# Seven-product groups summed in the accumulator banks, in all four groups of the first stage too

## The chip, the core and the metric

One core of a Trainium2 chip runs the whole program. The metric is the device time of one execution in microseconds (us). The kernel before takes 918.64 us (median of 3 runs, 917.53 to 919.39).

## What is computed

A trunk of two layers over x of 256 tokens by 1024 channels, all in float32. Each layer has a feed-forward stage, an attention mixer and a second feed-forward stage, so there are four feed-forward stages (stage 1 to 4 below):

```python
def swiglu(h, w_gate, w_up, w_down):
    return (jax.nn.silu(h @ w_gate) * (h @ w_up)) @ w_down
...
    for l in range(DEPTH):
        x = x + 0.5 * swiglu(rms_norm(x, ffn1_norm[l]), ffn1_w_gate[l], ffn1_w_up[l], ffn1_w_down[l])
...
        x = x + jnp.concatenate([out_a, out_b], axis=-1) @ w_out[l]
        x = x + 0.5 * swiglu(rms_norm(x, ffn2_norm[l]), ffn2_w_gate[l], ffn2_w_up[l], ffn2_w_down[l])
    return rms_norm(x, final_norm)
```

`w_gate` and `w_up` are 1024 x 2816, `w_down` is 2816 x 1024.

## The kernel before

**Products.** Each operand is kept as a high part and a low part (the rest), so that one product of 128x128 by 128x512 is three matmuls: high by high, low by high, high by low. The 2816 columns of gate and up are worked through in five groups of 512 columns (`NGRP = 5`, group 0 to 4) and a last one of 256. In a plain group gate and up each take the 256 tokens (two halves of 128) by the 1024 channels (two halves of 512), that is eight products of a 128-token half with a 512x512 quarter of the weights, each of 12 matmuls. In a group by seven (`SEVEN`, L31, and `by_seven`, L637) the four quarters A (gate, upper rows), B (up, upper), C (up, lower) and D (gate, lower) and the four quarters of x are combined as in Strassen's and Winograd's scheme: seven products, with A, D, B+C, C, A+B, A+B+C and A+B+C+D as weights, and sums of x's quarters (`make_sums`, L349, four of them, in `sm`) as the other factor. The results are put together by VectorE (`put`, L642: five combinations a group) from copies that ScalarE made (`m1`, `m7`). Stage 1 has groups 2 to 4 by seven, the other stages groups 1 to 4.

**Hidden units and down projection.** Gate goes through SiLU on ScalarE (`silu`, L603), is multiplied by up on VectorE (`up`, L614) and gives h, which PE transposes (`turn`, L694) and multiplies by two blocks of `w_down` (`down`, L708) during the next group; the sums of the down projection stay in four of PSUM's eight banks (`accs`, L706) through the stage.

**Weights.** `specs` lists all loads and splits as steps in the order of their use; a step of the usual kind is 1 MiB. `emit_dma` (L148) loads into one of six buffers (`raw`) on SP's queue; `emit_split` (L191) makes high and low parts by a cast on ScalarE and a subtraction on VectorE, two halves a step, of 1.05 and 1.22 us. B+C and A+B are made by accumulating DMAs on GpSimd's queue (`gather`, L126), which read the second weight from memory and add it to the loaded buffer; A+B+C and A+B+C+D are then made in place by VectorE (`plus`, L131).

**What sets the order.** Instructions on TensorE (PE), ScalarE (ACT), VectorE (DVE) and GpSimd (POOL) are kept in program order (`Kept`, L40). `weights()` (L249) hands out the next step and calls `ahead` (L228), which issues splits up to `2 * i + look` half steps ahead, and loads up to ten steps ahead while fewer than six buffers are held; the second half of a step's use calls `ahead` again (`Split.part`, L182) unless `held`. So at each such place, casts enter ACT's queue ahead of whatever the program issues afterwards. Accumulating DMAs may be kept back in `pending` (`issue`, L165: kind 2, C onto B, with B's load; kind 1, B onto A, after A's splits) while `hold` is at least their kind; `flush` (L171) issues them, the last one first. `hold` starts at 2; it is 1 from the end of every later feed-forward stage and mixer on. In stage 1 `flush` is called by `take_x` (L441 to 466) in its third part, after the squares of x, the statistics (`stats`, L397, whose last step r is on POOL) and `constants()` (L487), which puts eight small DMAs and some small work on POOL. In the other stages it is called by `late` (L592) behind the statistics.

**Group 0** (L712 to 746): two steps a0 and b0 in parts, then d0 and c0, 72 of the matmuls after the last part of x. With `1 in sevens` it also copies x for the sums (`norm.copies`, eight ACT instructions) and makes the sums.

Of the kernel before, what the change touches and what calls it, by code (L numbers as in the profile page):

```python
# [14 lines left out]
P = 128  # L15
# [15 lines left out]
SEVEN = ((2, 3, 4), (1, 2, 3, 4))  # L31
# [3 lines left out]
def trunk(ctx: ExitStack, tc: tile.TileContext, x, n1, g1, u1, d1, nm, w_in, sink,  # L35
# [35 lines left out]
    def bank():  # L71
        return ps.tile([P, 512], F32, tag="ps", bufs=8, name=nm_("ps"))
# [19 lines left out]
    class Step:  # L92
        def __init__(self, kn, n, moves, key=None, prep=None, src=None, free=None, behind=None):
            self.kn, self.n, self.moves, self.prep = kn, n, moves, prep
            self.behind = behind
# [19 lines left out]
    def seven(wg, wu, c0, downs, first):  # L115
# [15 lines left out]
        def plus(x, to):  # L131
            def prep():
                for h in (0, 2):
                    x_, t_ = [raws[i][:, h:h + 2] for i in (x, to)]
                    dve.tensor_tensor(t_, t_, x_, op=ALU.add)
# [92 lines left out]
    def ahead(n):  # L228

        n = min(n, 2 * len(specs) - 1)  # L230
        while True:
            if at["split"] <= n and at["prep"] > at["split"] // 2:
# [3 lines left out]
            elif at["prep"] <= min(n // 2 + 1, len(specs) - 1) and at["dma"] > at["prep"] and \  # L236
                    (specs[at["prep"]].prep is None or at["split"] >= 2 * at["prep"]):
# [21 lines left out]
    for l in range(DEPTH):  # L259
        def ffn_specs(wg, wu, wd, sevens):  # L260
# [3 lines left out]
            for g in range(1, NGRP):  # L264
                downs = [down(g - 1, h) for h in range(2)]
                if g in sevens:
                    specs.extend(seven(wg[l], wu[l], g * 512, downs, g == 1))
                else:
                    specs.extend(plain(w[l], g * 512, 512, k0, 4) for w in (wg, wu) for k0 in (0, 4))
                    specs.extend(downs)  # L270
# [35 lines left out]
    class Norm:  # L306
# [42 lines left out]
        def make_sums(self):  # L349
# [19 lines left out]
            s1 = add(b1, t1, ALU.subtract)  # L369
            s2 = add(s1, t0, ALU.add)  # L370
            yield
            high(s1)
            high(s2)
            yield
            low(0, s1)
            b0_ = add(b0, s2, ALU.subtract)
            low(1, s2)
            v = add(t1, t0, ALU.subtract)
            yield
            high(b0_)  # L380
            high(v)
            yield
            low(2, b0_)
            low(3, v)
# [145 lines left out]
    def tokens(accs, xs, w, k0, ks=range(4), first=0, last=KC - 1, order=None, cols=slice(None), h=None):  # L530

        for k, t in (order or [(k, t) for k in ks for t in range(2)]):
            kk = k0 + k
            hi, lo = w.part(k, cols, h)
            xv = xs[kk // 2][:, kk % 2]
            xh, xl = xv[:, t * P:(t + 1) * P], xv[:, S + t * P:S + (t + 1) * P]
# [23 lines left out]
    def first_groups(norm, ws):  # L560

        sls = [halves(bank()) for _ in ws]
# [39 lines left out]
    def ffn(norm, aside=None, before=None, final=False, sevens=SEVEN[1]):  # L602
# [34 lines left out]
        def by_seven(h, g):  # L637
# [3 lines left out]

            def put(o, x, y, op):  # L642
                dve.tensor_tensor(o, x, y, op=op)
                return o

            late, run = g == max(sevens), 1 in sevens
            m1, m7 = flat(), flat()


            if g > 1:  # L650
                g0 = prod(norm.quarter(0, 0), weights())
                act.copy(m1, g0)
                p7 = prod(norm.summed(3), weights(1, True))
                act.copy(m7, p7)
                hT = turn(h, 2)
                prod(norm.quarter(0, 1), weights(), g0)
                p3 = prod(norm.summed(2), weights())
                if not run:
                    g0 = silu(flat(), g0, 0)
                down(hT, g - 1, 0, weights())  # L660
                if run:
                    g0 = silu(flat(), g0, 0)
            else:
                p1 = prod(norm.quarter(0, 0), weights(1, True))
                hT = turn(h, (0,))
                w = weights(1, True)
                act.copy(m1, p1)
                p2 = prod(norm.quarter(0, 1), w)
                hT += turn(h, (1,))
                g0 = put(flat(), p2, m1, ALU.add)  # L670
                down(hT, 0, 0, weights())
                silu(g0, g0, 0)
                p3 = prod(norm.summed(2), weights())
                p7 = prod(norm.summed(3), weights(1, True))
                act.copy(m7, p7)
            h = blk(F32)
            p5 = prod(norm.summed(0), weights())
            prod(norm.summed(1), weights(look[0] - 5 if late else run, late or run), p7)
            u1 = put(m1, p7, m1, ALU.subtract)
            p4 = prod(norm.quarter(1, 1), weights(look[0] - 4 if late else 3 * run, late or run))  # L680
            g1 = put(flat(), p4, u1, ALU.subtract)
            w = weights(look[0] - 3 if late else 2 * run)
            silu(g1, g1, 1)
            put(u1, u1, p5, ALU.subtract)
            u0 = put(m7, u1, m7, ALU.subtract)
# [476 lines left out]
```

## Time and profile before

| | |
|---|---|
| median of 3 runs | 918.64 us |
| profiled execution | 917.39 us |
| its span, first to last instruction | 915.6 us |
| PE busy | 904.5 us (99%) |
| DVE busy | 792.5 us (87%) |
| ACT busy | 589.8 us (64%) |
| POOL busy | 66.4 us (7%) |
| bytes moved | 200.87 MB, mean 219 GB/s |

Stretches of the profile: group 0 of stage 1 up to about 31 us, its group 1 (plain) to 65 us, three groups by seven to 157 us, the end of the stage and the mixer to 284 us, stage 2 to about 457 us, stage 3 to about 633 us, the mixer to 734 us, stage 4 to the end.

All helpers issue through one line, so the rows of the profile nearly all read L50 and are told apart by engine, operation and tiles: `w<-raw` is a split, `ps<-w,s`, `ps<-w,q` and `ps<-w,v` are products (x in `s`, its sums in `q` and `v`), `ps<-ident,s` is a transposition of h, `raw<-in_ffn_w_up_dram` on POOL is an accumulating DMA, `junk<-xk` are the squares, `tmp<-ps,r` and `tmp<-tmp,r` are SiLU, `s<-ps,gcol` of 128x256 f32 are the copies of x for the sums. A row of the timeline gives start, duration, engine, instruction, count, and in brackets the idle time of the engine before it and what ended it. Times of a busy PE include a modelled tail of the last matmul.

### The profile page before, as it was taken

How to read it: one execution, taken by the hardware profiler on the slowest of the kernel's cores; microseconds unless marked ns; L12 is line 12 of the kernel's file. 1: busy time of each engine (PE TensorE's matmuls, PEld its weight loads, DVE VectorE, ACT ScalarE, POOL GpSimd, SP SyncE). 2: the span in 40 equal slices, each digit the busy share in tenths (PEclk: the TensorE clock that was granted, in tenths of full speed). 3: DMA queues.
4: the chain of work that ended last, by engine and by line, in shares of the span. 5: the costliest groups of instructions: out<-in, count | busy, mean ns of one | idle time of the engine just before them, and what ended most of it. 6: DMA issues, size and time to landing. Idle time of an engine off the chain costs nothing.

```text
span 915.6 us, 12544 instructions
## 1 busy us (share of the span) xinstructions
PE 904.5 (99%) x4696; PEld 763.7 (83%) x4696; DVE 792.5 (87%) x1096; ACT 589.8 (64%) x917; POOL 66.4 (7%) x83
## 2 busy tenths in 40 slices
PE   8999999999999999999999999999999999999997
PEld 6888888899888888888888888888998888888886
DVE  6768999959975999999789999997797689999994
ACT  7836676557865766576486666665677496666561
POOL 0400100000010100100010010000001010010011
PEclk9999999999999999999999999999999999999999
DMA  9996898828436698898767998887463467998831
GB/s 339 355 238 173 265 297 268 238 93 240 136 108 189 158 280 248 257 273 275 258 164 201 276 285 217 265 293 219 116 230 98 139 153 201 275 289 230 259 132 47
DMA packets 114061, 200.87 MB, mean 219 GB/s; under 512 B 3662, under 2 KB 31376, under 8 KB 114000
## 3 DMA queue, kind: packets, MB, share of 16 engines
q1 hardware_dynamic: 96528, 166.74, 54.5%
q0 software_dynamic: 16096, 31.75, 19.3%
q10 hardware_dynamic: 1376, 1.57, 0.5%
q8 instruction: 37, 0.61, 0.3%
q14 instruction: 24, 0.20, 0.1%
HBM read 199.00 MB, written 1.05 MB: 218 GB/s over the span
## 4 chain that ended last, share of the span: by engine, by line
PE 98%; issue 1%; DMA 0%; ACT 0%; DVE 0%; POOLq 0%; POOL 0%; ACTq 0%
PE ps L50 98%; DMA xk<-in_x_dram 0%; ACT w L50 0%; DVE s L50 0%; DVE xk L50 0%; ACT tmp L50 0%; ACT L50 0%; POOLq L1157 0%; POOL rf L50 0%; ACTq L50 0%; DVE tot L50 0%; DVE tmp L50 0%
## 5 line engine op out<-in xcount | busy, mean ns | idle before, releaser
L50 PE MATMUL ps<-w,s 128*128 128x512 f32 (+1 forms) x2574 | 600.2, 391 | 0.5 <-ACT tmp L50 0.5
L50 PEld LDWEIGHTS ps<-w,s 128*128 128x128 f32 x2574 | 477.6, 188 | 100.3 <-ACT tmp L50 2.3
L50 DVE TENSOR_TENSOR w<-raw,w 128x1024 fp32r<-128x1024 f32 (+1 forms) x458 | 482.1, 1101 | 37.8 <-ACT w L50 36.6
L50 ACT CAST w<-raw 128x1024 fp32r<-128x1024 f32 (+1 forms) x458 | 409.8, 954 | 122.6 <-DVE raw L50 78.4
L50 PE MATMUL ps<-w,q 128*128 128x512 f32 x540 | 127.3, 389 | 0.0
L50 PEld LDWEIGHTS ps<-w,q 128*128 128x128 f32 x540 | 101.4, 188 | 21.0
L50 PE MATMUL ps<-s,w 128*128 128x256 f32 x672 | 83.1, 284 | 0.0
L50 PEld LDWEIGHTS ps<-s,w 128*128 128x128 f32 x672 | 81.5, 192 | 0.5
L50 POOL DMA_DIRECT2D raw<-in_ffn_w_up_dram x30 | 38.9, 1296 | 472.8 <-DVE w L50 240.8
L50 DVE TENSOR_TENSOR raw<-raw,raw 128x1024 f32<-128x1024 f32 x60 | 70.7, 1219 | 0.0
L50 ACT ACTIVATE s<-ps,gcol 128x256 fp32r<-128x256 f32 (+1 forms) x80 | 31.7, 480 | 43.7 <-PE ps L50 42.1
L50 ACT CAST s<-ps 128x512 fp32r<-128x512 f32 x44 | 24.3, 594 | 29.9 <-PE ps L50 29.9
L50 PE MATMUL ps<-w,v 128*128 128x512 f32 x180 | 43.3, 389 | 0.0
L50 ACT COPY tmp<-ps 128x512 f32<-128x512 f32 x34 | 19.9, 585 | 36.2 <-PE ps L50 34.0
L50 ACT ACTIVATE s<-s,negm 128x256 f32<-128x256 f32 x64 | 31.9, 500 | 14.8 <-DVE negm L50 14.8
L50 PE MATMUL ps<-ident,s 128*128 128x128 f32 x304 | 39.7, 273 | 0.0
L50 PEld LDWEIGHTS ps<-w,v 128*128 128x128 f32 x180 | 33.8, 188 | 7.0
L50 PEld LDWEIGHTS ps<-ident,s 128*128 128x128 f32 x304 | 35.1, 140 | 5.1 <-issue 0.8
L50 DVE TENSOR_TENSOR s<-ps,s 128x512 fp32r<-128x512 f32 x44 | 28.7, 686 | 9.1 <-ACT s L50 9.1
L50 DVE SCALAR_TENSOR_TENSOR s<-ps,gcol,s 128x256 fp32r<-128x256 f32 x48 | 20.3, 478 | 11.6 <-ACT s L50 11.5
L50 DVE TENSOR_TENSOR tmp<-ps,tmp 128x512 f32<-128x512 f32 x37 | 25.4, 686 | 2.7 <-PE ps L50 2.1
L50 DVE TENSOR_TENSOR xk<-xk,ps 128x512 f32<-128x512 f32 (+1 forms) x25 | 14.1, 598 | 14.9 <-PE ps L50 14.9
(106 smaller groups left out, 404.7 us busy)
## 6 DMA issues: line engine op xcount, KB each, us to landing
raw<-in_ffn_w_down_dram SPq DMA_DIRECT2D x44, 1024.0 KB, 8.9
raw<-in_ffn_w_gate_dram SPq DMA_DIRECT2D x39, 1024.0 KB, 6.4
raw<-in_ffn_w_up_dram SPq DMA_DIRECT2D x39, 1024.0 KB, 5.7
raw<-in_ffn_w_up_dram POOLq DMA_DIRECT2D x30, 1024.0 KB, 12.3
raw<-in_w_in_dram SPq DMA_DIRECT2D x14, 1024.0 KB, 6.1
raw<-in_ffn_w_gate_dram SPq DMA_DIRECT2D x8, 512.0 KB, 6.2
raw<-in_ffn_w_up_dram SPq DMA_DIRECT2D x8, 512.0 KB, 7.2
raw<-in_w_in_dram SPq DMA_DIRECT2D x8, 512.0 KB, 5.3
```

The costliest lines, as they stand in the source:

```text
L50: ins = issue(*a, **k)
```

## The change

1. `SEVEN` gets group 1 in stage 1: `((1, 2, 3, 4), (1, 2, 3, 4))`.
2. `by_sevens` replaces `by_seven` and runs all groups of a stage in one loop. The products are added up in the banks: ScalarE copies the first product, negated, into both banks of a pair (`xy`), PE adds the third product into the first and the sixth into the second of them; the fifth is copied over the first product's bank, for the eighth step to add to; between the fifth product and the seventh, which goes on in the fifth's bank, stands the sixth. VectorE has three combinations a group left.
3. Order of a group's steps: A, the second down block of the group before the last, D, B+C, the first down block of the last group, A+B, C, A+B+C, A+B+C+D. (Before: A, B+C, D, C, down, A+B, A+B+C, A+B+C+D, down; as the first group of a stage A, D, down, C, B+C and so on.) h is transposed by tokens (`turn_one`), the first half after product A, the second after the down block.
4. PSUM: six single banks and one pair in place of eight; `accs` are taken when first used; the pair also serves group 0 (`us`), the last group and places in the mixer.
5. `make_sums` takes other signs and another order; `plus` is one instruction for a whole buffer, not two for halves, and may be issued one step earlier (`early`); a split of a summed step is not issued while an accumulation is pending (`added`).

`take_x`, `constants`, `issue`, `flush` and `hold` are as before.

```diff
-SEVEN = ((2, 3, 4), (1, 2, 3, 4))
+SEVEN = ((1, 2, 3, 4), (1, 2, 3, 4))
...
-        return ps.tile([P, 512], F32, tag="ps", bufs=8, name=nm_("ps"))
+        return ps.tile([P, 512], F32, tag="ps", bufs=6, name=nm_("ps"))
+    def pair():
+        return ps.tile([P, 2, 512], F32, tag="xy", bufs=1, name=nm_("xy"))
...
-        bc = Step(4, 512, load(b), key=b, behind=gather(c, b))
-        rest = [Step(4, 512, load(d), key=d, free=[]), Step(4, 512, load(c), key=c, free=[]), downs[0]]
-        steps = [rest[0], rest[2], rest[1], bc] if first else [bc] + rest
+        steps = [Step(4, 512, load(d), key=d, free=[]), Step(4, 512, load(b), key=b, behind=gather(c, b)), down]
+        if below is not None:
+            steps.insert(0, below)
         steps[0].prep = lambda: issue(gather(b, a), 1)
         return [Step(4, 512, load(a), key=a, free=[])] + steps + [
                 Step(4, 512, None, src=a, free=[]),
-                Step(4, 512, None, prep=plus(c, a), src=a, free=[c]),
-                Step(4, 512, None, prep=plus(d, a), src=a, free=[a, d]),
-                downs[1]]
+                Step(4, 512, load(c), key=c, free=[]),
+                Step(4, 512, None, prep=plus(c, a), src=a, free=[c], early=1),
+                Step(4, 512, None, prep=plus(d, a), src=a, free=[a, d])]
...
-            if at["split"] <= n and at["prep"] > at["split"] // 2:
+            if at["split"] <= n and at["prep"] > at["split"] // 2 and                     not (pending and specs[at["split"] // 2].added):
...
+            for g in groups:
+                start, late = old is None, g == groups[-1]
+                look[0] = lead(g)
+                p1 = prod(norm.quarter(0, 0), weights(start, start))
+                act.activation(xy, p1.unsqueeze(1).to_broadcast([P, 2, 512]), AF.Copy, scale=-1.0)
+                if start:
+                    g0 = flat()
+                    act.copy(g0, p1)
+                new = [turn_one(h, 0)]
+                if start:
+                    p2 = prod(norm.quarter(0, 1), weights())
+                    new.append(turn_one(h, 1))
+                    dve.tensor_tensor(g0, p2, g0, op=ALU.add)
+                    prod(norm.summed(0), weights(), xy[:, 0])
+                    below(by_token(new), g - 1, 0, weights(max(look[0] - 7, 0), True), [(k, t) for t in range(2) for k in range(4)])
+                    silu(g0, g0, 0)
+                else:
+                    below(old, g - 2, 1, weights())
+                    new.append(turn_one(h, 1))
+                    prod(norm.quarter(0, 1), weights(), p1)
+                    prod(norm.summed(0), weights(), xy[:, 0])
+                    below(by_token(new), g - 1, 0, weights(max(look[0] - 7, 0), True))
+                    g0 = silu(flat(), p1, 0)
+                old = by_token(new)
+                p5 = prod(norm.summed(1), weights(look[0] - 5, True))
+                act.copy(p1, p5)
+                prod(norm.summed(2), weights(max(look[0] - 7, 0) if late else 0, late), xy[:, 1])
+                prod(norm.summed(3), weights(look[0] - 5 if late else 1, True), p5)
+                e = flat()
+                act.copy(e, p5)
+                u1, u0 = flat(), flat()
+                dve.tensor_tensor(u0, xy[:, 1], e, op=ALU.add)
+                dve.tensor_tensor(u1, xy[:, 0], e, op=ALU.add)
+                h = blk(F32)
+                up(h, u0, g0, 0)
+                p4 = prod(norm.quarter(1, 1), weights(look[0] - 4 if late else 3, True), p1)
+                g1 = flat()
+                dve.tensor_tensor(g1, p4, u1, op=ALU.subtract)
+                if late:
+                    w = weights(look[0] - 3)
+                else:
+                    ahead(2 * at["use"] + look[0] - 2)
+                silu(g1, g1, 1)
+                up(h, u1, g1, 1)
+            below(old, groups[-1] - 1, 1, w)
             return h
```

More of the change, by code (lines that the diff above doesn't have):

```diff
@@ L560, in first_groups @@
     def first_groups(norm, ws):
-        sls = [halves(bank()) for _ in ws]
+        both = pair()
+        sls = [halves(both[:, i]) for i in range(2)]
         for k in range(0, KC, 2):
@@ L635, in prod @@
             return acc
-        def by_seven(h, g):
-            flat = lambda: tmp().rearrange("p a n -> p (a n)")
[L642 to L685, printed above, removed]
-            put(u0, u0, p3, ALU.add)
-            if run and g == max(sevens) - 1:
-                ahead(2 * at["use"] - 2 + look[0] - 1)
-            up(h, u0, g0, 0)
-            up(h, u1, g1, 1)
-            down(hT, g - 1, 1, w)
@@ L851, in q_finish, with scores @@
             return [q[:, 0], q[:, 1]]
-        def scores(q, kb, dist, slopes, init, den):
-            sl = [bank(), bank()]
+        def scores(q, kb, dist, slopes, init, den, wide=False):
+            both = pair() if wide else None
+            sl = [both[:, i] if wide else bank() for i in range(2)]
             for t in range(2):
@@ L937, in mix @@
         vB = tp.tile([P, 2, 512], F32, tag="v", bufs=1, name=nm_("v"))
-        vsl = [bank() for _ in range(2)]
+        both = pair()
+        vsl = [both[:, t] for t in range(2)]
         for k0 in (0, 4):
@@ L984, in mix @@
         oT = [blk() for _ in range(4)]
-        rsl, osl = [[bank() for _ in range(2)] for _ in range(2)]
+        rsl, both = [bank() for _ in range(2)], pair()
+        osl = [both[:, t] for t in range(2)]
         for t in range(2):
```

92 lines of the change are left out of this document (60 added, 32 removed).

## The prediction

> **What bounds the kernel now.** I read the page's head and its chain first, then PE's waits.
>
> ```profile
> span 915.6 us, 12544 instructions
> PE 904.5 (99%) x4696; PEld 763.7 (83%) x4696; DVE 792.5 (87%) x1096; ACT 589.8 (64%) x917; POOL 66.4 (7%) x83
> PE 98%; issue 1%; DMA 0%; ACT 0%; DVE 0%; POOLq 0%; POOL 0%; ACTq 0%
> ```
> ```profile
> PE ps L50 <- ACT tmp L50: 0.5, 1, 0.5
> ```
>
> PE is busy 99% and is 98% of the chain; after the start it waits for another engine once, 0.5 us. So PE's own work sets the time, and whatever keeps PE waiting is added in full. DVE is next. The stretches below are each exactly one group of a stage (84 matmuls of seven products, 48 of two quarters of the down projection, 8 transposes); the columns are length, then busy time by engine.
>
> ```profile
> 368.99:399.80 30.81, 30.81 (x141) 25.61 (x140) 30.30 (x31) 20.16 (x24) 2.57 (x2) 1.00 0.94 263
> 575.59:606.75 31.16, 31.16 (x142) 25.45 (x140) 30.47 (x32) 20.31 (x25) 0.22 (x1) 1.00 0.86 269
> 848.93:880.31 31.38, 31.38 (x142) 25.37 (x140) 30.27 (x32) 19.87 (x24) 0.49 (x1) 1.00 0.79 243
> ```
>
> DVE works 30.3 of 30.8 us, ACT 20. The last groups of stages 3 and 4 take 0.35 and 0.57 us longer than the first of these rows for the same instructions: there DVE's splits arrive late. That is all that DVE costs.
>
> **The change, part by part.** *One product less.* Group 1 of the first stage goes from eight products of 12 matmuls to seven.
>
> ```profile
> 319.11 2.88 PE L50 MATMUL ps<-w,q 128*128 128x512 f32 x12
> 321.83 2.88 PE L50 MATMUL ps<-w,v 128*128 128x512 f32 x12
> ```
>
> Start to start a product is 321.83 - 319.11 = 2.72 us: **-2.72**. In all other groups the matmuls and transposes are as many as before.
>
> *Sums in the banks.* Per group two of five DVE combinations go and ACT copies more: 1024 elements into the pair, 512 bank to bank, 512 out (two copies of 512 before).
>
> ```profile
> L50 DVE TENSOR_TENSOR tmp<-ps,tmp 128x512 f32<-128x512 f32 x37 | 25.4, 686 | 2.7 <-PE ps L50 2.1
> L50 ACT COPY tmp<-ps 128x512 f32<-128x512 f32 x34 | 19.9, 585 | 36.2 <-PE ps L50 34.0 <-DVE w L50 2.1
> ```
>
> DVE gives back 2 x 0.69 = 1.4 us a group, more than the 0.92 us that it costs in two groups: **-0.9** (bounds 0 and -0.9, since PE cannot gain more). ACT gets 1.2 (if the wide copy takes one row's time) to 1.8 us (twice) more in a group where it idles 10: nothing, as long as ACT is not stuck. The copy between the fifth product and the seventh has the sixth, 2.72 us, beside it; uncovered it would cost some 0.6. In attention the pair serves one user after another; I bound this by 0 and +2 and take 0.
>
> *The first stage's group 1, loads and queues.* Here I expect the time to go. Group 0's work in the first stage:
>
> ```profile
> 13.97 16.61 PE L50 MATMUL ps<-w,s 128*128 128x512 f32 x72
> 18.57 6.10 ACT L50 CAST w<-raw 128x512 fp32r<-128x512 f32 x8
> 24.57 0.63 ACT L50 ACTIVATE junk<-xk 128x512 f32<-128x512 f32 x1
> 25.10 0.19 ACT L50 ACTIVATION_READ_ACCUMULATOR junk<-xk 128x1 f32 x1
> 26.28 0.15 DVE L50 TENSOR_REDUCE ms<-nss 128x2 f32<-128x4 f32 x1
> 26.79 0.72 POOL L50 TENSOR_TENSOR r<-ms,mhalf 128x2 f32<-128x2 f32 x1 [25.29 <-DVE ms L50]
> 31.39 0.54 POOL L50 DMA_DIRECT2D s<-in_lam_k_dram  x1
> 38.23 3.04 ACT L50 ACTIVATE s<-ps,gcol 128x256 f32<-128x256 f32 x8
> 39.19 0.46 POOL L50 TENSOR_TENSOR s<-s 128x128 f32<-128x128 f32 x1 [1.52 <-DMA s<-in_lam_k_dram]
> 43.40 1.38 POOL L50 DMA_DIRECT2D raw<-in_ffn_w_up_dram  x1 [3.75 <-ACT w L50]
> ```
>
> By the new order of steps, group 1 loads A, D and B, and B is summed with C by an accumulating DMA of POOL before it is split. `hold` is still 2 in this stage, so both accumulations (B onto A, C onto B) stay pending until `flush()`, which `take_x` calls after `constants()`. Later stages hold only B onto A; there C onto B leaves with B's load. On POOL's queue `constants()` is the series from r (26.79) to the last product, which waits for a small DMA and ends at 39.65. In the new kernel the eight copies for the sums (38.23, 3.04 us) stand on ACT ahead of the squares (24.57); 1.0 us of that is covered, since the squares end with their read-out at 25.10 + 0.19 and the reduction over them starts at 26.28, so r and the series come 2.0 later: 41.7, or 39.7 if the small DMAs land faster with fewer loads beside them. I take 40.7. `pending` is emptied from its end, so B onto A goes first.
>
> ```profile
> q0 software_dynamic: 16096, 31.75, 19.3%
> raw<-in_ffn_w_up_dram POOLq DMA_DIRECT2D x1, 1024.0 KB, 8.4
> raw<-in_ffn_w_up_dram POOLq DMA_DIRECT2D x2, 1024.0 KB, 14.7
> ```
>
> These rows are POOL's whole queue, then the accumulations issued in 466:473 (nearly alone) and in 40:52 (beside loads). All 30 take 0.193 x 915.6 / 30 = 5.9 us each of the 16 engines. The first lands at 40.7 + 8.4 = 49.1, the second 5.9 later: **55.0**. Bounds: 39.7 + 1.3 + 8.4 = 49.4, if both run fully beside each other, and 41.7 + 1.3 + 14.7 = 57.7. The Trainium skill, "DMA: Bandwidth & Descriptors", section "Anatomy of one DMA — SWDGE (gpsimd) path", fits 2.0 us plus bytes over 436e3 to a GpSimd DMA; for 1 MiB that is 4.4 us, an estimate by which the pair would land some 6 us sooner. The row's 8.4 decides, since these DMAs also add.
>
> Why does PE wait for it? `weights()` of the third step puts both splits of BC on ACT's queue, in program order ahead of the sums' high parts and of SiLU of group 0, without which there is no h to transpose. The trace shows ACT stuck so:
>
> ```profile
> 50.00:55.00 5.00, 5.00 (x24) 4.14 (x23) 1.11 (x2) 0.00 (x0) 0.29 (x1) 1.00 1.09 259
> ```
> ```profile
> 57.86 2.00 ACT L50 CAST w<-raw 128x1024 fp32r<-128x1024 f32 x2 [10.60 <-DMA raw<-in_ffn_w_up_dram]
> ```
> ```profile
> 333.26 2.95 ACT L50 CAST w<-raw 128x1024 fp32r<-128x1024 f32 x3 [2.94 <-DMA raw<-in_ffn_w_up_dram]
> 336.12 0.71 ACT L50 ACTIVATE tmp<-tmp,r 128x512 f32<-128x512 f32 x1
> ```
>
> At 47 to 57.86 ACT did nothing for 10.6 us until BC of group 2 landed; at 333.26 a SiLU stands behind such casts. Both were hidden by PE's store of split weights. Group 1 of the first stage has none. After BC lands come its two casts (2.00), then what stage 2 shows for the same steps:
>
> ```profile
> 288.98 1.34 POOL L50 DMA_DIRECT2D raw<-in_ffn_w_up_dram  x1 [29.44 <-DVE w L50]
> 300.65 1.08 POOL L50 TENSOR_TENSOR r<-ms,mhalf 128x2 f32<-128x2 f32 x1 [10.34 <-DVE ms L50]
> 301.71 1.32 POOL L50 DMA_DIRECT2D raw<-in_ffn_w_up_dram  x1
> ```
> ```profile
> 301.19 1.35 ACT L50 CAST q<-tmp 128x512 fp32r<-128x512 f32 x2
> 302.45 1.99 ACT L50 CAST w<-raw 128x1024 fp32r<-128x1024 f32 x2
> 304.46 1.28 ACT L50 ACT_TABLE_LOAD   x1
> 305.76 1.27 ACT L50 ACTIVATE tmp<-ps,r 128x512 f32<-128x512 f32 x2
> 307.69 1.41 DVE L50 SCALAR_TENSOR_TENSOR s<-ps,hr,tmp 128x512 f32<-128x512 f32 x2
> ```
>
> (The POOL rows show the hold: C onto B left at 288.98, B onto A directly behind r.) From the first high part to the first half of h, 301.19 to 307.69 + 0.7, is 7.2 us. So PE has h at 55.0 + 2.0 + 7.2 = 64.2. It ran out at the end of its 72 matmuls, 13.97 + 16.61 = 30.6 less the last one's tail of 0.16 (2.88 - 2.72), plus product A's 2.72: 33.1. **+31.1.** Everything later on PE shifts with it. The 0.5 us wait of before goes, as the new kernel has free banks there: **-0.5**.
>
> *A cold array.* The kernel's first matmuls were slow:
>
> ```profile
> 6.47 5.74 PE L50 MATMUL ps<-w,s 128*128 128x512 f32 x19
> ```
>
> 19 x 0.227 (2.72 / 12) + 0.16 = 4.5 us, against 5.74: **+1.3** if 31 idle us bring that back; bounds 0 and 1.7. The Trainium skill, "TensorE: Matmul & The Clock Gate", section "Part 1: The HAM clock gate", has the array fall to half rate after an idle window of some 3.4 us and need as long to recover. By that the cost is an estimate of 1.7; if the gate did not fall, 0. The granted clock in the windows reads 1.00 in the first microseconds too, so that column can't tell.
>
> **Sum:** -2.72 - 0.9 - 0.5 + 31.1 + 1.3 = +28.3. The profiled execution took 917.39 us (its span 915.6 and 1.8 around it), 1.25 under the median of the runs; 918.64 + 28.3 = **947**.
>
> **The rivals.** *No stall* (the other side, faster): the pair lands before PE reaches h, which decides at 33.1 - 9.2 = 23.9 us. Then only -2.72 - 0.9 - 0.5 are left: 914.5. For it: DMA and POOL have idle time. Against: POOL is at 26.79 with r alone. The point would be reached only if `flush` came ahead of r. Chance 0.12; a cover of all but 2 us gives no change, 0.02.
>
> *The bank's product alone waits*: ACT gets SiLU done ahead of the casts, and PE stops at product BC, behind A, D (5.44) and two turns of four transposes.
>
> ```profile
> 309.98 0.60 PE L50 MATMUL ps<-ident,s 128*128 128x128 f32 x4
> ```
>
> A turn is 0.60 less the tail, 0.44; so PE stops at 30.4 + 5.44 + 0.88 = 36.7, until 55.0 + 2.4 for a cast and a low part. That is 20.7 in place of 31.1: 937. Against: 333.26 shows casts and SiLU in queue order. Chance 0.10.
>
> *Later stages wait too*: the second half of h now is turned 2.72 + 5.44 + 0.44 = 8.6 us after a group's last product, and its SiLU stands behind BC's first cast of the next group, whose accumulation starts when C's buffer comes free. Row 333.26 shows the cast at the moment of landing. If it is 3 us late in the first group of three stages, 9 more: 956; in nine groups, 27: 974. For: an accumulation takes 8 to 15 us. Against: PE uses BC 9 us later in a group than before. Chance 0.14.
>
> **Numbers.** The forecast, 935 to 956 by the landing's bounds (-5.6, +2.7), the cold term, attention and a few us of late splits after the stall, has 0.62. With the two slower-side rivals up to 963 and down to 932 the range holds 0.8. Faster by over 0.2% 0.12, within 0.2% (about what a measurement of this kernel can tell from no change) 0.02, slower 0.86.
>
> **What would show it.** In the new profile: PE idle for some 31 us from about 33 us, its wait put down to ACT or DVE; an ACT row with a wait of over 20 us for the DMA of the up weights; two accumulations issued back to back at 40 to 43 us on POOL, behind the constants; PE with 12 fewer 512-wide matmuls; seven-product groups of 30.8 us in all stages, the last ones too; DVE near 29 us in each. Wrong it would be if the accumulations left before r, or if PE's idle time lies in stages 2 to 4.

## The result and the profile after

The changed kernel takes 975.68 us (median of 4 runs, 974.11 to 979.32) against 918.15 us of the kernel before in the same session (917.53 to 919.39). The ratio is 1.063, with a 95% interval of 1.0595 to 1.0666. The forecast was 947 us with a range of 932 to 963: the direction is right, the size is not. The profiled execution took 977.08 us, its span 975.3: 59.7 us more than the span before.

The page of the changed kernel, its head and its chain:

```profile
span 975.3 us, 12408 instructions
PE 915.4 (94%) x4684; PEld 765.3 (78%) x4684; DVE 782.0 (80%) x1048; ACT 609.4 (62%) x945; POOL 65.8 (7%) x85
PE 52%; DVE 19%; DMA 15%; ACT 8%; issue 4%; POOL 1%; POOLq 0%; ACTq 0%; DVEq 0%
```

PE was 98% of the chain and is 52% of it now; DVE, the DMAs and ACT stand in it. The 12 matmuls are gone (4684 against 4696). PE's waits (us in total, how many, the longest):

```profile
PE ps L50 <- DVE s L50: 46.8, 16, 23.3
```

One wait of 23.3 us, and fifteen that share the other 23.5. The first is where the forecast put it. PE, ACT and POOL in the first stage:

```profile
31.31 2.88 PE L50 MATMUL ps<-w,s 128*128 128x512 f32 x12
57.46 1.12 PE L50 MATMUL ps<-ident,s 128*128 128x128 f32 x4 [23.27 <-DVE s L50]
58.23 4.54 PE L50 MATMUL ps<-w,s 128*128 128x512 f32 x12
```
```profile
29.58 1.01 POOL L50 TENSOR_TENSOR r<-ms,mhalf 128x2 f32<-128x2 f32 x1 [28.08 <-DVE ms L50]
...
39.41 0.46 POOL L50 TENSOR_TENSOR s<-s 128x128 f32<-128x128 f32 x1 [0.34 <-DMA s<-in_lam_k_dram]
40.11 2.70 POOL L50 DMA_DIRECT2D raw<-in_ffn_w_up_dram  x2 [0.25 <-issue]
```
```profile
48.63 1.99 ACT L50 CAST w<-raw 128x1024 fp32r<-128x1024 f32 x2 [19.60 <-DMA raw<-in_ffn_w_up_dram]
...
54.87 1.27 ACT L50 ACTIVATE tmp<-ps,r 128x512 f32<-128x512 f32 x2
```

The two accumulations leave back to back at 40.11, behind the constants; ACT stands 19.60 us until BC lands, and only then come the casts, the table and SiLU. That is the forecast's picture, with an earlier landing. Behind the wait PE's 12 matmuls take 4.54 us where 2.88 is usual.

The fifteen others lie in the later groups, where the forecast had none. The window from one first turn to the next in the second group of the second and the third stage (length, then busy time of PE, PEld, DVE, ACT, POOL, then the granted clock, the busy share of the DMA engines, and GB/s):

```profile
367.23:404.78 37.55, 33.87 (x142) 27.34 (x140) 29.95 (x29) 22.51 (x27) 2.57 (x2) 0.91 0.88 247
553.65:589.21 35.56, 32.86 (x142) 26.47 (x140) 29.93 (x29) 22.62 (x27) 2.57 (x2) 0.95 0.88 256
```

DVE works no more than before (29.9 us a group against 30.3), and yet a group of 30.8 us takes 35.6 to 37.6. Inside the first of these windows, PE, ACT and DVE:

```profile
367.23 0.60 PE L50 MATMUL ps<-ident,s 128*128 128x128 f32 x4
367.58 5.72 PE L50 MATMUL ps<-w,s 128*128 128x512 f32 x24
376.79 1.12 PE L50 MATMUL ps<-ident,s 128*128 128x128 f32 x4 [3.49 <-DVE s L50]
```
```profile
369.76 1.05 ACT L50 CAST w<-raw 128x1024 fp32r<-128x1024 f32 x1 [4.49 <-DMA raw<-in_ffn_w_up_dram]
370.72 0.72 ACT L50 ACTIVATE tmp<-tmp,r 128x512 f32<-128x512 f32 x1
371.34 2.93 ACT L50 CAST w<-raw 128x1024 fp32r<-128x1024 f32 x3
374.17 1.01 ACT L50 ACTIVATE xy<-ps 128x1024 f32<-128x1024 f32 x1
375.11 0.58 ACT L50 CAST s<-ps 128x512 fp32r<-128x512 f32 x1
```
```profile
371.99 0.74 DVE L50 SCALAR_TENSOR_TENSOR s<-tmp,hr,tmp 128x512 f32<-128x512 f32 x1
372.65 3.49 DVE L50 TENSOR_TENSOR w<-raw,w 128x1024 fp32r<-128x1024 f32 x3
376.05 0.68 DVE L50 TENSOR_TENSOR s<-ps,s 128x512 fp32r<-128x512 f32 x1
```

The second half of h is ready at 372.7, but the second turn starts at 376.79. What it waits for is a bank: outside the down projection's four accumulators and the pair, two banks rotate; one holds the new group's first product, the other the first turn, and it is free only when ACT's copy (375.11) and DVE's low part (376.05) have read it. Both stand in their queues behind splits, and ACT's queue stood 4.49 us for BC.

Counted from start to start of PE's instructions against their usual pitch (0.227 us for a 512-wide matmul), the 59.7 us are about 52.7 of waits (more than the wait rows say, as those count from the end of a pipelined matmul), 7.2 of matmuls at about 0.43 us, 2.7 less for the product, and 2.5 of small rests.

### The profile page after: what moved, and what is told of

Same layout as the page of the kernel before. It is cut to its first block, busy times and chain, and to the rows that moved or that the text cites. A ratio compares the mean times of both kernels' runs of the same rounds, so it can differ in the third digit from the quotient of the medians.

```text
span 975.3 us, 12408 instructions
## 1 busy us (share of the span) xinstructions
PE 915.4 (94%) x4684; PEld 765.3 (78%) x4684; DVE 782.0 (80%) x1048; ACT 609.4 (62%) x945; POOL 65.8 (7%) x85
## 4 chain that ended last, share of the span: by engine, by line
PE 52%; DVE 19%; DMA 15%; ACT 8%; issue 4%; POOL 1%; POOLq 0%; ACTq 0%; DVEq 0%
PE ps L50 38%; PE xy L50 14%; DMA raw<-in_ffn_w_up_dram 14%; DVE w L50 12%; ACT w L50 4%; DVE raw L50 3%; ACT s L50 2%; DVE s L50 2%; DVE tmp L50 1%; DMA s<-in_lam_k_dram 0%; DMA xk<-in_x_dram 0%; DVE q L50 0%; ACT xy L50 0%; ACT ps L50 0%; ACT tmp L50 0%
## 5 line engine op out<-in xcount | busy, mean ns | idle before, releaser
L50 PE MATMUL ps<-w,s 128*128 128x512 f32 (+1 forms) x2034 | 488.3, 395 | 3.9 <-DVE s L50 3.4
L50 PEld LDWEIGHTS ps<-w,s 128*128 128x128 f32 x2034 | 381.4, 191 | 85.2 <-DVE s L50 4.7
L50 PE MATMUL xy<-w,s 128*128 128x512 f32 x480 | 114.2, 391 | 0.0
L50 PEld LDWEIGHTS xy<-w,s 128*128 128x128 f32 x480 | 89.4, 188 | 18.4
L50 PE MATMUL xy<-w,q 128*128 128x512 f32 x384 | 92.8, 390 | 0.0
L50 PEld LDWEIGHTS xy<-w,q 128*128 128x128 f32 x384 | 71.9, 188 | 15.0
L50 DVE TENSOR_TENSOR raw<-raw,raw 128x2048 f32<-128x2048 f32 x32 | 73.2, 2288 | 0.5
L50 PE MATMUL ps<-s,w 128*128 128x256 f32 x480 | 59.3, 284 | 0.0
L50 PE MATMUL ps<-w,q 128*128 128x512 f32 x192 | 46.1, 389 | 0.0
L50 PEld LDWEIGHTS ps<-w,q 128*128 128x128 f32 x192 | 36.0, 188 | 7.5
```

The costliest lines, as they stand in the source:

```text
L50: ins = issue(*a, **k)
```

## The experiments

A result with a ratio is the median of four or five executions; one without is the time of a single execution.

**Where the loss lies.** The theory now has two places, each about half: the first stage's group 1, and the later groups. The rival is the forecast's own, group 1 alone.

*Group 1 by eight products again.*

```diff
-SEVEN = ((1, 2, 3, 4), (1, 2, 3, 4))
+SEVEN = ((2, 3, 4), (1, 2, 3, 4))
```

> One part undone: group 1 of the first stage goes by eight products again, and all other groups stay by seven with the sums in the banks. Theory of two places: the wait of 23.4 us at 33.8 us goes with some 2 us of slow matmuls behind it, 12 matmuls (2.72 us) come back, and the waits of the later groups stay: about 953 us. Rival, as forecast before the result: all the loss is in group 1 of the first stage, so without it the kernel is at 917 - 0.9 = about 916 us.

946.81 us, ratio to before 1.0303 (1.0276 to 1.033). Group 1 of the first stage was worth 975.7 - 946.8 = 28.9 us: its wait, the slow matmuls behind it, and most of what followed in groups 2 to 4 of that stage, which was not expected to go; why those groups recover was not tested. The other 28.6 us are in the later groups. The forecast's place is half of the story.

```profile
PE ps L50 <- DVE s L50: 19.1, 14, 2.5
```

*The accumulations ahead of the constants.*

```diff
-            constants()
             flush()
+            constants()
```

> The two pending accumulations leave POOL's queue before the constants and not behind them. Theory: BC of the first stage's group 1 waits for POOL's place in the queue, so the accumulations leave 9.6 us sooner (30.5 instead of 40.1), the wait of 23.4 us shrinks to about 14, and the time is about 966 us, with every later group's waits as they were. Rival: BC waits for the DMA engines, which are busy with loads until 35 us; then the wait stays over 20 us and the time over 972.

965.93 us, ratio 1.0516 (1.0479 to 1.0554). POOL, PE and ACT of this run:

```profile
30.28 2.81 POOL L50 DMA_DIRECT2D raw<-in_ffn_w_up_dram  x2
```
```profile
48.74 1.12 PE L50 MATMUL ps<-ident,s 128*128 128x128 f32 x4 [15.06 <-DVE s L50]
```
```profile
39.91 1.99 ACT L50 CAST w<-raw 128x1024 fp32r<-128x1024 f32 x2 [11.16 <-DMA raw<-in_ffn_w_up_dram]
```

The place in POOL's queue is worth what it was said to be: 9.8 us earlier on POOL, 8.7 earlier on ACT and PE, 9.8 off the time. The wait that is left, 15 us, is the accumulation itself and what stands behind it on ACT.

**The later groups, one suspect at a time.** The first two were built on the changed kernel, those after them on the one of 946.8 us.

*ACT's copies ahead of BC's casts.*

```diff
-                p1 = prod(norm.quarter(0, 0), weights(start, start))
+                p1 = prod(norm.quarter(0, 0), weights(1 if start else 4, True))
...
                 new = [turn_one(h, 0)]
+                if not start:
+                    ahead(2 * at["use"] - 1 + look[0])
```

> Only the order on ACT is changed, in groups 2 to 4 of each stage: the copy into the pair and the copy of the first turn are issued ahead of the second half of BC's casts and the casts behind it, instead of behind them. The accumulations, the banks and the number of instructions stay. Theory: the waits of 1 to 3.7 us before the second turn (22.0 us in twelve groups, and some 5 us of slow matmuls behind the longest) come from those copies standing behind a cast that waits for the accumulation; they go, and the time is about 975.7 - 27 = 949 us. Rival 1: two rotating banks are too few or DVE is too late, whatever the order on ACT: unchanged, 973 to 976. Rival 2: the accumulation is late for PE itself, so the wait moves to product BC: 965 to 976, with PE waiting in the BC product.

971.83 us, ratio 1.0575 (1.0558 to 1.0592): 4 us of the 27. The theory of this run falls. The time lies in rival 2's range, but its picture is not what is seen either. The waits before second turns did go, and PE then waited elsewhere:

```profile
PE ps L50 <- DVE s L50: 33.5, 11, 24.0
PE ps L50 <- DVE tmp L50: 7.5, 8, 1.2
```

The row DVE tmp is a first turn waiting for a bank that DVE still has to read (the last product's combination), and 33.5 - 24.0 = 9.5 us are matmuls of the down projection waiting for a turn's low part. Of these, three waits of 1.15 us in first groups were there before; the other 6 us are new, as the low part now came later.

*BC without its accumulation.*

```diff
-        if s.behind is not None:
-            issue(s.behind, 2)
```

> C is never added onto B, so product BC multiplies with B alone (this part of the computation is left out); everything else stays, the order on ACT too. Theory: BC's casts then wait for B's load alone, which in the second stage's group 2 lands at 355.4 where the accumulation lands at 369.7; the later groups' waits go (22 us, and some 5 of slow matmuls), and in the first stage's group 1 the wait of 23.4 us shrinks to some 6 us for AB, whose accumulation is still behind the constants: about 931 us. Rival, banks or DVE: only the first stage's part goes, about 958 us.

958.97 us: the rival's number. In the first stage the wait fell to 4.6 us, with another of 4.9 for a turn's copy behind AB's casts; the second stage's group 2 kept most of its wait (2.54 us against 3.49), without any DMA in it. Its ACT, DVE and PE:

```profile
353.92 0.72 ACT L50 ACTIVATE tmp<-tmp,r 128x512 f32<-128x512 f32 x1 [1.35 <-DVE tmp L50]
354.55 2.93 ACT L50 CAST w<-raw 128x1024 fp32r<-128x1024 f32 x3
```
```profile
353.81 3.48 DVE L50 TENSOR_TENSOR w<-raw,w 128x1024 fp32r<-128x1024 f32 x3
357.21 0.74 DVE L50 SCALAR_TENSOR_TENSOR s<-tmp,hr,tmp 128x512 f32<-128x512 f32 x1
357.88 3.48 DVE L50 TENSOR_TENSOR w<-raw,w 128x1024 fp32r<-128x1024 f32 x3
361.28 0.68 DVE L50 TENSOR_TENSOR s<-ps,s 128x512 fp32r<-128x512 f32 x1
```
```profile
362.02 1.12 PE L50 MATMUL ps<-ident,s 128*128 128x128 f32 x4 [2.54 <-DVE s L50]
```

So the queue's order is enough: SiLU is done at 354.6, but DVE has three low parts ahead of the product with it and three more ahead of the turn's low part, 7 us of work for others. The Trainium skill says in "Perfetto Trace Analysis", section "Tensor Engine Instruction (MATMUL, LD_WEIGHTS)", that ACT, DVE and GPSIMD take their instructions strictly in order; these rows agree.

*Two more banks.* Both output halves of the down projection accumulate in the same two banks.

```diff
-                accs.append([bank(), bank()])
+                accs.append(accs[0] if accs else [bank(), bank()])
...
-            tokens(accs[h], of, w, 4 * g, last=(FC - 1, G4 - 1) if final and h else FC - 1, order=order)
+            tokens(accs[h], of, w, 4 * g, last=(FC - 1, G4 - 1) if final and h else FC - 1, order=order, first=-1 if h else 0)
```

> Built on the kernel with group 1 of the first stage by eight (946.8 us). Both halves of the down projection accumulate in the same two banks (so the output halves are mixed: this part of the computation is left out), which leaves four rotating banks for products and turns and not two. Instructions and their order on every engine stay. Theory: the matmuls of a turn wait for a bank, which is free only when DVE's low part of the turn before has come through its queue; with two more banks the waits before turns go (17.0 us, 1.1 before first turns, some 5.5 of slow matmuls behind them), the waits of 1.31 us in the first groups stay, since there a product waits for the low part itself: about 923 us. Rival: turns wait for the second half of h, which is late in DVE's queue, and not for a bank: 940 us or more.

944.34 us, 2.5 us less, which is within the spread of the four runs that it is measured against (945.57 to 949.17); the rival's range. PE's waits:

```profile
PE ps L50 <- DVE s L50: 11.0, 16, 1.2
PE ps L50 <- ACT xy L50: 2.7, 6, 0.6
```

The longest wait fell from 2.5 to 1.2 us, and the slow matmuls went with it, but new waits stand in their place, among them for ACT's copy into the pair. Banks alone are not the cause.

*No additions on DVE.*

```diff
-                dve.tensor_tensor(raws[to], raws[to], raws[x], op=ALU.add)
+                pass
```

> Built on the same kernel. DVE's two additions of whole buffers in each group (2.29 us each) are left out, so the last two products of a group use wrong weights; that part of the computation is left out. Theory: a wait is set by what stands ahead of the one short operation in DVE's queue. The 1.31 us waits of the first groups go, since an addition stands there; the turns wait behind low parts of splits and keep most of their waits: 935 to 943 us. Rival: DVE has too much work altogether (80% of the span, near all of a group), so 4.6 us less in each group ends every wait: about 918 us.

938.5 us, as the theory had it: the waits of the first groups (1.31 us from start to start, 1.15 in PE's rows) are gone, those before second turns stayed as they were (2.4 us, the longest, against 2.5), though DVE had 4.6 us less to do in each group. DVE's amount of work is not what bounds a group.

```profile
PE ps L50 <- DVE s L50: 13.3, 10, 2.4
```

*Turns side by side and late, with the four banks* (the edit of the run with two more banks is in it too).

```diff
-                new = [turn_one(h, 0)]
+                new = [turn_one(h, 0)] if start else []
...
-                    new.append(turn_one(h, 1))
                     prod(norm.quarter(0, 1), weights(), p1)
+                    new = [turn_one(h, t) for t in range(2)]
```

> Built on the kernel with group 1 of the first stage by eight (946.8 us). As in the run with two more banks, both halves of the down projection accumulate in the same two banks (output halves mixed, which leaves that part out), so four banks rotate. With them the turns of a later group are put where the kernel before had them, both side by side behind the products A and D and the down product, some 11 us after the group before has ended, and not at 2.7 and 8.6 us. The loads and their order, the splits and the sums in the pair stay. Theory: the pair's two banks cost because two rotating banks force the turns to be early and apart, where the short operations stand behind splits; with four banks and late turns, waits of 17 us before turns and most of the slow matmuls go and no others come: about 923 us. Rival: what is late is the splits themselves, with the accumulations, and the wait moves to the products: 935 to 945.

976.82 us, 30 us slower, outside both ranges. The down product now waits for the low parts of both turns (29.0 us in 14 waits by DVE s, the longest 3.6; three of them, of 1.15 us, are the old ones of the first groups), as they stand behind splits and an addition on DVE. The place that the kernel before gave its turns is no remedy in the new order.

*First groups alone.*

```diff
-                    p2 = prod(norm.quarter(0, 1), weights())
+                    p2 = prod(norm.quarter(0, 1), weights(3, True))
                     new.append(turn_one(h, 1))
+                    ahead(2 * at["use"] - 1 + look[0])
```

> Built on the same kernel; nothing is left out. Only in the first group by seven of a stage the splits issued with the second product are issued behind the copies of the second turn and not ahead of them. Theory: the wait of 1.31 us in three stages is for the second turn's low part, which stands behind an addition (2.28 us) and a split's low part (1.21) in DVE's queue; it goes, and the time is about 946.8 - 3.9 = 943 us. Rival: the splits that now come later are missed by the products of the same group: unchanged or slower, 946 to 950.

954.48 us, ratio 1.039 (1.0369 to 1.0411): 7.7 us slower, not 3.9 faster, and outside both ranges. The 1.31 us waits went; the splits that were put off came back in the next group, in the third stage as

```profile
527.53 0.66 PE L50 MATMUL ps<-ident,s 128*128 128x128 f32 x4 [2.25 <-DVE s L50]
...
537.34 1.11 PE L50 MATMUL ps<-ident,s 128*128 128x128 f32 x4 [3.67 <-DVE s L50]
```

**Order and buffers together.** The whole order: second halves of splits behind the copies of each turn, the first turn in the middle of the down product, the next down product token by token; the first group's edit above and the hold of the run with ACT's copies ahead are in it too.

```diff
+                if not start:
+                    w = weights(6, True)
+                    below(old, g - 2, 1, w, [(k, t) for k in range(2) for t in range(2)])
                 new = [turn_one(h, 0)]
...
-                    below(old, g - 2, 1, weights())
+                    ahead(2 * at["use"] - 3 + look[0])
+                    below(old, g - 2, 1, w, [(k, t) for k in range(2, 4) for t in range(2)])
                     new.append(turn_one(h, 1))
-                    prod(norm.quarter(0, 1), weights(), p1)
+                    prod(norm.quarter(0, 1), weights(2), p1)
...
-                    ahead(2 * at["use"] + look[0] - 2)
+                    ahead(2 * at["use"] + look[0] - 3)
```

> Built on the same kernel; nothing is left out, only the order is changed in groups by seven. In groups after a stage's first, the first turn stands in the middle of the down product and not ahead of it, the second behind it as before, the splits of BC and later steps are issued behind each turn's copies on ACT and DVE, BC's first cast no longer stands ahead of SiLU, and the next down product goes token by token. In a stage's first group the splits are issued behind the second turn's copies. Theory: waits come from short operations of ACT and DVE behind splits in their queues, and two banks do if these go first: waits of 22 us and some 5.5 of slow matmuls go: about 919 us, at best 915. Rival 1: two rotating banks are too few in any order: 935 or more. Rival 2: the splits are now too late and the products wait for weights: 930 or more, with PE waiting for DVE's w.

952.28 us, ratio 1.0362 (1.0344 to 1.0379): 5.5 us slower, and rival 2's waits. No wait for DVE s is left in PE's list; weights are late instead. PE's waits, and ACT in the second stage:

```profile
PE ps L50 <- DVE w L50: 7.3, 13, 1.3
PE ps L50 <- ACT tmp L50: 5.4, 6, 1.4
PE ps L50 <- ACT w L50: 4.6, 8, 0.7
```
```profile
354.68 3.91 ACT L50 CAST w<-raw 128x1024 fp32r<-128x1024 f32 x4 [3.62 <-DMA raw<-in_ffn_w_up_dram]
```

With the turns out of the way, ACT waits for AB's accumulation.

*One more load buffer*, with that order and without it:

```diff
-N_RAW, N_S4 = 6, 28
+N_RAW, N_S4 = 7, 26
```

> The kernel of the run with the turns spread, with seven load buffers and 26 tiles for split weights in place of 6 and 28. Theory: once the turns wait for nothing, the splits are late because B's load gets its buffer late and so both accumulations leave 5 us later (333.9 and 340.0 against 328.6 and 335.7 in the second stage) and land 12 to 15 us after that; one more buffer lets B's load and the accumulations go some 5 us sooner, and the waits for weights (ACT w, DVE w: some 15 us) shrink: about 935 us. Rival: the late splits come from ACT's and DVE's own queues and the additions, so the buffer changes nothing or the missing two tiles cost: 950 to 958.

> The kernel with group 1 of the first stage by eight (946.8 us), its order untouched, with seven load buffers and 26 tiles for split weights in place of 6 and 28. It parts the gain of the run that had both this buffer and the spread turns (929.6 us) from that of the order. Theory: in this order the turns wait for short operations behind splits in the queues, whatever the loads do, so the 17 us before turns and the 3.9 us of the first groups stay: 940 to 948 us. Rival: the late accumulations alone make the splits and all behind them late, and the buffer does it without the order: about 930 us.

With the order 929.59 us, 22.7 less, more than expected; without it 941.03, 5.8 less, as expected, with the waits before turns as they were. With the order, the waits for weights shrink to

```profile
PE ps L50 <- DVE w L50: 2.3, 4, 1.3
```

and none for ACT w is left. Waits for a copy by ACT (ACT tmp, 4.3 us in four) stay.

So order and buffer are worth 17.2 us together, but -5.5 and 5.8 alone: the gain of each shows only with the other.

*The seventh product's copy ahead of later splits*, in two steps; the first also runs the first stage's splits one half step further ahead.

```diff
-                prod(norm.summed(3), weights(look[0] - 5 if late else 1, True), p5)
+                prod(norm.summed(3), weights(look[0] - 5 if late else look[0] - 3, True), p5)
                 e = flat()
                 act.copy(e, p5)
+                if not late:
+                    ahead(2 * at["use"] - 3 + look[0])
```
```diff
-                prod(norm.summed(2), weights(max(look[0] - 7, 0) if late else 0, late), xy[:, 1])
+                prod(norm.summed(2), weights(max(look[0] - 7, 0) if late else look[0] - 5, True), xy[:, 1])
```

> The kernel with spread turns and seven buffers (929.6 us), nothing left out, with two more changes of order: the copy of the seventh product out of its bank is issued ahead of the next group's splits on ACT and not behind four of them, and in the first stage the splits run one half step further ahead. Theory: the waits of 1.53 us for that copy in three stages go, with those of 0.3 us before first turns, and the 3.0 us of waits for splits in the first stage: about 922 us, 4 above the kernel before, whose stalls and slow matmuls this order then shares. Rival: the splits issued later are late for the next group's down product, and the waits come back as waits for w: 927 to 932 us.

> The kernel of 926.4 us with one more change of order: in groups after a stage's first and before its last, the step of C's product issues no splits beyond the same group, so that two casts and not six stand on ACT ahead of the copy of the seventh product. Theory: the three waits of 1.53 us for that copy go, and those of 0.3 us after them shrink: about 921.5 us. Rival: two rotating banks make PE wait in any order, and the wait comes back elsewhere: 925 to 928.

926.39 us (ratio 1.0085, 1.0068 to 1.0101) and 926.09 us (1.0083, 1.0069 to 1.0097), where 922 and 921.5 were expected. The first ended the first stage's waits and left the copy where it was, behind six casts. The second moved the copy, its wait went, and first turns waited in its place, as this run's rival said of the time and of the wait. The largest entry behind the start in PE's list of the second, and one of its windows:

```profile
PE ps L50 <- DVE tmp L50: 2.5, 6, 0.5
```
```profile
340.41:372.43 32.02, 31.53 (x140) 25.33 (x141) 29.51 (x28) 21.67 (x26) 2.57 (x2) 1.00 0.91 262
```

The group of 37.6 us is back at 32.0, with the pair and two rotating banks. Of the 28.6 us in the later groups 20.7 were thus order and loads. The last 8 stay open: waits in PE's list explain 2.7 of them (7.5 us in all against 4.8 before). Counted from start to start as above, waits hold about 4 us more than before, slow or late single matmuls 2.5 and smaller rests the remainder, and that two banks cost this was not shown.

*Group 1 by seven once more*, with the accumulations ahead of the constants, BC's casts behind SiLU and the turns' copies, and BC's load and product behind the down product's.

```diff
-SEVEN = ((2, 3, 4), (1, 2, 3, 4))
+SEVEN = ((1, 2, 3, 4), (1, 2, 3, 4))
...
-            constants()
             flush()
+            constants()
...
-                look[0] = IN_FFN + (1 in sevens)
+                look[0] = IN_FFN + (1 in sevens) if before is not take_x else 6
...
+                    if before is take_x:
+                        below(by_token(new), g - 1, 0, weights(0, True), toks)
+                        prod(norm.summed(0), weights(0, True), xy[:, 0])
```

> The kernel of the run beside it, with group 1 of the first stage by seven products again (12 matmuls less), but with both accumulations on POOL's queue ahead of the constants, BC's casts behind SiLU and both turns' copies on ACT, and BC's product behind the down product and not ahead of it. Theory: the stall of 23.4 us came from the place in two queues and not from the sum itself; the accumulations leave at about 30.5 us, BC lands at about 39 and PE needs it at about 42, h is ready at about 34.5, so that PE waits 1 to 2 us there and not 23: 0 to 2 us under the run beside it, about 920.5. Rival: both accumulations run beside the loads at 30 to 45 us and land after 45, so PE waits 5 us or more: 924 to 930.

937.68 us, ratio 1.0212 (1.0197 to 1.0227), against 926.09 beside it on the same chip, and outside both ranges. The order did what it should; the DMA did not. POOL, ACT and PE:

```profile
30.55 2.83 POOL L50 DMA_DIRECT2D raw<-in_ffn_w_up_dram  x2 [1.54 <-ACT q L50]
```
```profile
43.23 2.00 ACT L50 CAST w<-raw 128x1024 fp32r<-128x1024 f32 x2 [4.15 <-DMA raw<-in_ffn_w_up_dram]
51.29 3.89 ACT L50 CAST w<-raw 128x1024 fp32r<-128x1024 f32 x4 [6.06 <-DMA raw<-in_ffn_w_up_dram]
```
```profile
34.62 0.66 PE L50 MATMUL ps<-ident,s 128*128 128x128 f32 x4
...
52.39 4.19 PE L50 MATMUL ps<-w,q 128*128 128x512 f32 x8 [4.24 <-ACT w L50]
```

PE turns h at 34.62 now, not at 57.46. But the two accumulations, issued at 30.55 beside the loads, reach ACT after 12.7 and 20.7 us, and AB comes 4.2 us too late. A product of 2.72 us is saved and some 14 are lost; from start to start 9.7 of these are waits (4.4 of them the one for AB) and 3.4 slow matmuls, most of them behind that wait. No version here beats the kernel before.

## Why the forecast was right in part and wrong in size

- *What bounds it.* Right that any wait of PE is added in full. Wrong was the use made of it: the 10 us that ACT idles in a group were read as slack, and DVE's full queue was priced at 0.92 us in two groups, when one wait of 0.5 us in PE's list showed only that the short operations came in time in the order before.
- *One product less, -2.72.* As forecast.
- *Combinations on DVE, -0.9.* DVE did lose a little work (29.9 us a group against 30.3), but the splits in the last groups were not what was late afterwards; no gain is seen.
- *ACT's copies at nothing, "as long as ACT is not stuck".* Here the forecast failed: it put the later groups at nothing, and they cost 28.6 us. It counted ACT's idle microseconds in a group, and not who waits for the copies: they free one of only two banks that rotate, and they and DVE's low parts stand behind splits. Of the 28.6 us, 20.7 went with order and one load buffer; what the last 8 are is open. The forecast named idle time of PE in stages 2 to 4 as a sign that it was wrong, and that sign came.
- *Group 1 of the first stage, +31.1.* The mechanism is as forecast, link by link: accumulations held until behind the constants (40.7 forecast, 40.11), casts on ACT ahead of SiLU, PE stopped at 33.1 (34.2). The mis-sized term is the landing: 55.0 forecast, and ACT's casts started at 48.63. The forecast, and the description of `flush` ahead of it, read that pending accumulations are taken from the end of the list, but the code takes the oldest first (`pop(0)`), and that is C onto B, which was added with B's load. Its own figure for the first of the two, 49.1, was close. From cast to turn it gave 9.2 us and 8.8 were measured. So 31.1 loses 6.4 for the landing, 1.1 for PE's later stop and 0.4 for that chain, and the wait is 23.3 us. That the forecast's terms for this group add up to 29.2 and the run with eight products puts it at 28.9 is luck: the wait was 7.8 shorter, and waits in groups 2 to 4 of the stage, which the forecast did not have, made up for most of it.
- *A cold array, +1.3 (0 to 1.7).* At that place 4.54 - 2.88 = 1.7. But waits in later groups brought slow matmuls back three more times; in all they cost about 7 us.
- *The 0.5 us wait of before.* Gone, as forecast; another, of 0.4 us for DVE w, stands at 179 us.
- *Attention, 0 (0 to +2).* In the kernel of 946.8 us two waits for ACT s hold 0.6 us that the kernel before does not have.
- *The rivals.* "Later stages wait too" came true, and at its full size: priced at 956 in three groups and 974 in nine, against 975.7 measured (a shorter first wait, longer ones behind it). It had 0.14, as PE "uses BC 9 us later", and the range was cut at 963. That its number came so close is luck: it named SiLU behind BC's first cast, 3 us in each of nine groups; the runs show the turn's bank and DVE's low parts instead, in fifteen waits of 0.8 to 3.5 us, and that a late landing is not needed for them. "No stall" and "the product alone waits" did not happen; the last run made the second happen, with AB in BC's place.

## What to carry to other kernels

Where one engine is busy 99% of the time, a change of order is priced by the queues of the others: for each short operation that this engine waits for, add up what stands ahead of it on ACT and DVE, and count the banks that rotate. When one suspect after another is taken away and the wait only moves, look for two limits at once, here the order and the load buffers, and change both. And a rival that would repeat in every group is to be weighed by its full price.

## What was not expected of the hardware

Short waits slow PE down afterwards. In the kernel of 946.8 us, fourth stage:

```profile
880.63 0.65 PE L50 MATMUL ps<-ident,s 128*128 128x128 f32 x4 [1.90 <-DVE s L50]
881.04 4.58 PE L50 MATMUL ps<-w,s 128*128 128x512 f32 x12
```

After a wait of 1.9 us twelve matmuls take 4.58 us and not 2.88, and the granted clock (the third number from the end) halves with them:

```profile
882.00:884.00 2.00, 2.00 (x6) 1.53 (x6) 0.00 (x0) 0.00 (x0) 0.00 (x0) 0.50 1.04 348
```

In the changed kernel the column reads 0.50 from 38 to 61 us, through the long wait and the slow matmuls behind it. So in these places the column does tell, where the forecast, going by the first microseconds, took it that it can't. The Trainium skill, "TensorE: Matmul & The Clock Gate", section "Part 1: The HAM clock gate", gives an idle window of some 3.4 us for the fall to half rate; here 1.9 us were enough, though not always, and after waits of 1.6 us and less no such run of slow matmuls is seen.

An accumulating DMA of 1 MiB is slowed by its neighbours: the first of the pair at 40.11 was taken up by ACT after 8.5 us, that of the pair at 30.28, with loads beside it until about 33 us, after 9.6, and that of the pair at 30.55, with loads until about 35 us, after 12.7. And it moves less: with the pair alone on the DMA engines of the changed kernel these are as busy as with plain loads, but move 208 GB/s (the last number), where loads at 30 to 33 us move 367.

```profile
45.00:48.00 3.00, 0.00 (x0) 0.00 (x0) 0.00 (x0) 0.00 (x0) 0.00 (x0) 0.50 1.13 208
```
